# Tokens and weights of a matmul: their distance modulo 256 bytes, and the order of the chunks, made to change from block to block

## The chip, the cores and the metric

The kernel runs on one core of one Trainium2 chip. The metric is device time in microseconds (us) of one execution; lower is better. A core has a matrix engine (TensorE, PE in the profile; its weight loads are listed apart as PEld), a vector engine (VectorE, DVE), an activation engine (ScalarE, ACT), a general engine (GpSimd, POOL) and a queue engine (SyncE, SP), which issues most of the transfers from the chip's memory (HBM) into the on-chip memory SBUF. SBUF has 128 partitions; all addresses below are byte addresses within a partition.

## The reference

One inference step of a decoder layer over 256 prompt tokens and 8 sample tokens, 264 columns in all, with a model width of 2048:

```python
xn = rmsnorm(x, g_mix);  z = xn @ w_in                      # 2048 -> 5128
y_rg = rmsnorm(rglru(conv(z...)) * gelu(z...))               # recurrent group
y_ml = rmsnorm(mlstm(q, k, v, i, f)) * sigmoid(z...)         # matrix-memory group
x = x + concat([y_rg, y_ml]) @ w_out
q = rmsnorm(x) @ w_xa_q;  k, v = mn @ w_xa_k, mn @ w_xa_v    # mn = rmsnorm(mem_prompt), prompt alone
x = x + attention(q, k, v) @ w_xa_o                          # samples use a cache of keys and values
x = x + (silu(xf @ w_ffn_gate) * (xf @ w_ffn_up)) @ w_ffn_down   # xf = rmsnorm(x), width 5632
y = rmsnorm(x)
```

Inputs and outputs are float32. Nearly all the arithmetic is in the products with the weight matrices.

## The kernel before

Activations lie transposed: features on the partitions, 264 tokens along the free dimension. A product with 2048 inputs and 128 outputs is a **block** or step: 16 chunks of 128 inputs, summed in one PSUM bank. To keep float32 precision from the matrix engine's faster float32r format, both operands are split into a high and a low part, and `mm3` (lines 179 to 184) issues three matmuls for each chunk: high weights by high tokens, high weights by low tokens, low weights by high tokens. The weights are the stationary operand (128 columns, loaded anew for each matmul) and the tokens the moving one (264 columns). A block is therefore 48 matmuls.

The list `steps` (line 137) holds all the blocks in order: `w_in`, `w_out`, `w_q`, then for each of 4 heads four blocks of `w_k` and four of `w_v`, then `w_o`, and the feed-forward, which comes in three parts (gate and up blocks in turn, `w_gu`, then 16 down blocks, `w_d`; the last part's down blocks have 12 chunks). `load_piece` (142) loads a block's weights, 1 MB as one transfer, into one of three `raw` buffers of 2048 elements. `split_half` (150) makes the high and low parts of one half, 8 chunks: ScalarE copies `raw` to `wh` with rounding to float32r, VectorE subtracts it from `raw` into `wl`. Both `wh` and `wl` have four buffers of 1024 elements, so two blocks' worth. The buffer of a half is free for a later half when the matrix engine has read all of its chunks.

Token arrays are made by `Arr` (110): four chunks to a tile `[128, 4, 264]` of the shared pool `B`, high and low parts in arrays of their own (`HL`). One chunk is 1056 bytes, which is 4 x 256 + 32, and a tile 4224 bytes, which is 16 x 256 + 128. A chunk of weights in `wh` or `wl` is 512 bytes, two times 256.

Around the blocks, other work (gates, recurrences, the samples' attention over the cache, `dec_k` and `dec_v`) is issued by generators that `pump` runs after each block, on VectorE, ScalarE and GpSimd; results of a block are taken from PSUM in the next step (`pend` in the main loop, 1233 to 1268). A scheduler orders the instructions of each engine; the transfers of SP stay in the order in which they are written.

Of the kernel before, what the change touches and what calls it, by code (L numbers as in the profile page):

```python
# [10 lines left out]
F32 = mybir.dt.float32  # L11
F32R = mybir.dt.float32r
# [5 lines left out]
P = 128  # L18
# [62 lines left out]
def layer_kernel(ctx: ExitStack, tc, xT, memT, vec, wrg, w_in, w_out, w_q, w_k, w_v, w_o,  # L81
# [10 lines left out]
    ctx.enter_context(tc.manual_schedule(engines={mybir.EngineType.SP}))  # L92

    uid = [0]

    def nm(s):
# [10 lines left out]
    def ltmp(w=N):  # L107
        return tmp(w, "lt")

    class Arr:  # L110


# [24 lines left out]
    steps = []  # L137
    LD, LS = 3, 1

    raws, splits = {}, {}  # L140

    def load_piece(i):
        if i >= len(steps) or i in raws:
            return
        src, cols = steps[i][0], steps[i][1]
        r = sb.tile([P, 2048], F32, tag="raw", bufs=3, name=nm("raw"))
        sp.dma_start(r[:, :cols], src)
        raws[i] = r

    def split_half(i, h, parts=1):  # L150
        if i >= len(steps):
            return
        if steps[i][2] is pe_if:
            if h == 0:
                split_gates(i)
            return
        cols = steps[i][1]
        lo, hi = h * 1024, min(cols, (h + 1) * 1024)
        wh = sb.tile([P, 1024], F32R, tag="wh", bufs=4, name=nm("wh"))
        wl = sb.tile([P, 1024], F32R, tag="wl", bufs=4, name=nm("wl"))  # L160
        r = raws[i]
        n = (hi - lo) // parts
        with tc.high_priority():
            for o in range(0, hi - lo, n):
                st["split"] = act.activation(wh[:, o: o + n], r[:, lo + o: lo + o + n], AF.Copy)
                dve.tensor_sub(wl[:, o: o + n], r[:, lo + o: lo + o + n], wh[:, o: o + n])
        splits[i, h] = (wh, wl)

    class W:
        def __init__(self, i):  # L170
            self.i = i

        def __call__(self, c, w=P):
            per = 1024 // w
# [60 lines left out]
    def bank(tag="mm"):  # L235
        return psm.tile([P, 512], F32, tag=tag, bufs=4, name=nm(tag))

    warm_act = const.tile([P, 1], F32, name="warm_act")
    act.activation(warm_act, ones[:, 0:1], AF.Square)

    def warm(n, w=None):
# [263 lines left out]

    def split_gates(i):

        r = raws[i]
        for h in range(2):
            w = sb.tile([P, 8, P], F32R, tag="wh", bufs=4, name=nm("wh"))  # L510
            x = r[:, h * 1024: h * 1024 + 1024].rearrange("p (c m) -> p c m", m=P)
# [610 lines left out]
    for h in range(H):  # L1122
        for j in range(4):
            proj(w_k[4 * h + j], rm, evac_k(h, j), n=T, need=("memg",))
        for k4 in range(4):
            steps.append((w_v[h, k4], 2048, pe_v(h, k4), evac_vm(h) if k4 == 3 else None, ()))

    def ro(c):
        return st["o"](c)
# [6 lines left out]
    def pe_o(m):  # L1136
        def f(i):
            ps = bank()
            w = W(i)
            if m >= 2:  # L1140
                for c in range(KC):
                    mm3(ps[:, :N], w(c), ro(c), c == 0, c == KC - 1)
                return ps
            held[m] = (ps, w)
            for c in range(12):
                mm3(ps[:, :N], w(c), ro(c), c == 0, False)
            if m == 0:
# [17 lines left out]
        return g  # L1165

    for m in range(KC):
        steps.append((w_o[m], 2048, pe_o(m), evac_xo(m), (("att", 2), "dk", "dv") if m == 0 else ()))


# [40 lines left out]
    def load_x(lo, hi):  # L1211
        sp.dma_start(xres[:, lo:hi, :], xT[:, lo:hi, :])

    r = sb.tile([P, 2048], F32, tag="raw", bufs=3, name=nm("raw"))
    raws[0] = r
    for h in range(4):
        if h < 2:
            load_x(2 * h, 2 * h + 2)
        sp.dma_start(r[:, h * 512: h * 512 + 512], w_in[0][:, h * 512: h * 512 + 512])
    for q in range(1, 4):  # L1220
        load_x(4 * q, 4 * q + 4)
        if q < 3:
# [157 lines left out]
```

## Time and profile before

| | before |
|---|---|
| median of 3 runs | 1575.6 us (1570.88 to 1576.71) |
| profiled execution: time | 1576.51 us |
| its span | 1574.8 us |
| granted clock of the matrix engine, mean | 0.991 |
| PE busy, instructions | 1556.5 us, 12340 |
| DVE busy | 1051.4 us |
| ACT busy | 789.7 us |
| read from HBM | 312.78 MB |

The profile's page lists, for one execution, the busy time of each engine, the time line in 40 slices, the transfer queues, the chain of work that ended last (followed back from the last instruction), and the costliest groups of instructions. Matmuls are pipelined: a matmul of 264 columns is listed with a duration of 285 ns, though the next begins some 121 ns after it. What counts for the matrix engine is therefore the time from start to start, which is read from a stretch and the number of matmuls in it.

### The profile page before, as it was taken

Reading aid. Unit: us, or ns where it says so; the run is one execution under the profiler, and the core shown is the slowest. Engines: PE = TensorE matmul, PEld = TensorE weight load, DVE = VectorE, ACT = ScalarE, POOL = GpSimd, SP = SyncE. Lnnn points to the kernel's source line nnn. Section 1 sums busy time; section 2 is a strip of 40 time slices with the busy share of each in tenths; the row PEclk is TensorE's granted clock in tenths of the full one; section 3 lists DMA queues with packets and bytes.
Section 4 is the critical chain, followed back from the end, with each engine's and each line's share of the span. In section 5 each row is a group of like instructions: output and inputs, shape, how many; then the busy total and the mean of one; then the engine's idle time right before and its main releaser. Section 6 shows DMA issues by size and latency. Waiting matters only on the chain.

```text
span 1574.8 us, 29829 instructions
## 1 busy us (share of the span) xinstructions
PE 1556.5 (99%) x12340; PEld 1532.6 (97%) x12340; DVE 1051.4 (67%) x2021; ACT 789.7 (50%) x1252; POOL 109.6 (7%) x174
## 2 busy tenths in 40 slices
PE   9999999999999999999999999999999999999997
PEld 8999999999999889999999999999999999999997
DVE  7876877787699899956655555455555554555554
ACT  7465675565455656645444444333444433344463
POOL 0001210000124333200000000000000000000000
PEclk9999999999999999999999999999999999999998
DMA  8455875546689788745545555555455554555452
GB/s 304 161 174 172 294 269 205 178 145 245 248 321 346 302 305 319 251 161 178 187 164 185 188 180 175 181 188 186 174 179 186 187 181 172 184 188 184 156 179 99
DMA packets 55303, 325.97 MB, mean 207 GB/s; under 512 B 6688, under 2 KB 7120, under 8 KB 24448
## 3 DMA queue, kind: packets, MB, share of 16 engines
q1 hardware_dynamic: 39744, 270.68, 48.4%
q0 software_dynamic: 15136, 53.16, 9.4%
q8 instruction: 96, 1.57, 0.4%
q14 instruction: 39, 0.32, 0.1%
q10 hardware_dynamic: 288, 0.23, 0.1%
HBM read 312.78 MB, written 11.28 MB: 206 GB/s over the span
## 4 chain that ended last, share of the span: by engine, by line
PE 94%; DMA 2%; DVE 2%; ACT 1%; issue 1%; DVEq 0%; POOL 0%; SPq 0%; ACTq 0%
PE mm L60 89%; PE ax L60 4%; DVE B L60 1%; DMA o_sc<-B 1%; ACT B L60 1%; DMA raw<-w_in 1%; ACT wh L60 0%; DMA B<-scr 0%; DVE wl L60 0%; ACT L60 0%; DMA vecs<-vec 0%; DMA scr<-lt 0%; DVE t L60 0%; DVE dw L60 0%; ACT t L60 0%
## 5 line engine op out<-in xcount | busy, mean ns | idle before, releaser
L60 PE MATMUL mm<-B,wh 128*128 128x264 f32 (+1 forms) x7520 | 1379.0, 285 | 4.8 <-DVE B L60 3.0
L60 PEld LDWEIGHTS mm<-B,wh 128*128 128x128 f32 x7520 | 1168.4, 189 | 6.4 <-ACT cso L60 3.1
L60 PE MATMUL mm<-B,wl 128*128 128x264 f32 (+1 forms) x3744 | 1062.8, 284 | 0.6 <-DVE wl L60 0.6
L60 ACT ACTIVATE wh<-raw 128x1024 fp32r<-128x1024 f32 (+2 forms) x518 | 536.9, 1038 | 692.0 <-PE mm L60 574.6
L60 DVE TENSOR_TENSOR wl<-raw,wh 128x1024 fp32r<-128x1024 f32 (+2 forms) x516 | 619.0, 1201 | 356.7 <-ACT wh L60 350.0
L60 PEld LDWEIGHTS mm<-B,wl 128*128 128x128 f32 x3744 | 706.7, 189 | 1.1 <-DVE wl L60 1.0
L60 DVE TENSOR_TENSOR t<-mm,rstd 128x264 f32<-128x264 f32 x104 | 44.9, 432 | 60.2 <-PE mm L60 60.2
L60 PE MATMUL mm<-wh,B 128*128 128x512 f32 x256 | 82.3, 395 | 0.0
L60 DVE TENSOR_TENSOR xres<-xres,mm 128x264 f32<-128x264 f32 x80 | 34.2, 428 | 47.1 <-PE mm L60 47.1
L1272 POOL TENSOR_TENSOR B<-B,rstd 128x264 f32<-128x264 f32 x4 | 2.8, 743 | 864.9 <-ACT rstd L60 864.9
L60 PEld LDWEIGHTS mm<-wh,B 128*128 128x128 f32 x256 | 47.8, 189 | 9.8
L60 DVE SCALAR_TENSOR_TENSOR B<-B,dw 128x256 f32<-128x256 f32 x128 | 52.6, 465 | 2.3 <-ACT dw L60 2.3
L60 PE MATMUL mm<-wl,B 128*128 128x512 f32 x128 | 50.6, 395 | 0.0
L60 DVE SCALAR_TENSOR_TENSOR dw<-B,qsm,dw 128x256 f32<-128x256 f32 x96 | 47.9, 500 | 1.4 <-ACT dw L60 0.7
L60 PE MATMUL ax<-B,B 128*128 128x256 f32 (+3 forms) x288 | 48.2, 308 | 0.3 <-DVE B L60 0.3
L60 PEld LDWEIGHTS ax<-B,B 128*128 128x128 f32 x288 | 40.8, 189 | 4.0 <-issue 1.2
L977 POOL TENSOR_TENSOR ds<-dw,ds 128x256 fp32r<-128x256 f32 x32 | 35.4, 1107 | 115.3 <-ACT ds L60 115.2
L60 ACT ACTIVATE B<-xres,vecs 128x264 fp32r<-128x264 f32 (+1 forms) x64 | 31.1, 503 | 2.5 <-DMA xres<-xT 1.4
L60 ACT ACTIVATE t<-xres 128x264 f32<-128x264 f32 x60 | 23.9, 413 | 15.4 <-DVE xres L60 15.4
L60 PEld LDWEIGHTS mm<-wl,B 128*128 128x128 f32 x128 | 24.1, 188 | 5.0
L966 POOL DMA_DIRECT2D B<-kcT x32 | 17.5, 546 | 147.4 <-DVE B L60 127.0
L60 DVE TENSOR_TENSOR acc_x<-acc_x,t 128x264 f32<-128x264 f32 x59 | 25.2, 428 | 0.9 <-ACT t L60 0.5
(157 smaller groups left out, 740.0 us busy)
## 6 DMA issues: line engine op xcount, KB each, us to landing
raw<-w_gu SPq DMA_DIRECT2D x88, 1024.0 KB, 4.8
raw<-w_in SPq DMA_DIRECT2D x40, 1024.0 KB, 4.9
raw<-w_d SPq DMA_DIRECT2D x32, 1024.0 KB, 4.8
raw<-w_out SPq DMA_DIRECT2D x16, 1024.0 KB, 4.8
B<-kcT POOLq DMA_DIRECT2D x32, 512.0 KB, 6.1
raw<-w_q SPq DMA_DIRECT2D x16, 1024.0 KB, 5.0
B<-vcT POOLq DMA_DIRECT2D x32, 512.0 KB, 7.2
raw<-w_k SPq DMA_DIRECT2D x16, 1024.0 KB, 6.4
```

Source lines behind the costliest of these rows:

```text
L60: return f(*a, **k)
L966: pool_e.dma_start(kc, kcT[h, b])
L977: pool_e.tensor_sub(ws[:, 1], acc, ws[:, 0].bitcast(F32))
L1272: e.tensor_mul(st["y"](c), st["y"](c), r)
```

## The change

In words:

- A half of a block now has one tile `w` of 2176 elements (four buffers) in place of `wh` and `wl`. It is used with a row of 264 elements for each chunk, 1056 bytes as for the tokens: elements 0 to 127 of a row are the high part, 128 to 255 the low part, which is 512 bytes on. The tokens' tiles are 1088 elements (4352 bytes, 17 x 256), and every second tile of an array begins 32 elements later, so that chunk after chunk goes on at 1056 bytes modulo 256. So the distance of a token chunk to its weights modulo 256 bytes is one number for a whole block.
- `scanned` lists the blocks of 16 chunks by 264 columns that wait for nothing of their own: 191 of them, counted in order from 0 (4, 8, 8 and 8 of `w_in`, 15 of `w_out`, 15 of `w_q`, 14 of `w_o`, 31, 32 and 24 of `w_gu`, 16 and 16 of `w_d`). For number k, `place` gives three values: a stride of the chunks (1 for k below 64, 7 below 128, then 3), an offset `a = k // 8 % 8` in units of 32 bytes for the weights, and a rotation `j = k % 8`: the low part of chunk c lies in row (c + j) modulo 8. `order` gives the chunks as stride x k modulo 16.
- Because of the rotation the subtraction of a half is cut in two where j is not 0.
- `w_k` and `w_v` blocks (`wide`) keep 1024 high elements in a row, with the low ones 1056 elements after the start. Blocks that are not scanned use a = 0, j = 0 and the plain order.
- Weights are loaded in halves of 512 KB, into five `raw` buffers of 1024 elements (before: three of 2048).

```diff
+    BW = 4 * N + 32
+    WO, WW = 48, 8 * N + 64
...
         def tile(self, q):
             if q not in self.t:
-                self.t[q] = B([P, min(4, self.nb), self.w], self.dt)
+                t, o = B([P, BW], self.dt), 32 * (q % 2) if self.w == N else 0
+                self.t[q] = t[:, o: o + 4 * self.w].rearrange("p (c n) -> p c n", n=self.w)
...
-        r = sb.tile([P, 2048], F32, tag="raw", bufs=3, name=nm("raw"))
-        sp.dma_start(r[:, :cols], src)
-        raws[i] = r
+        raws[i] = []
+        for o in range(0, cols, 1024):
+            r = raw_half()
+            w = min(1024, cols - o)
+            sp.dma_start(r[:, :w], src[:, o: o + w])
+            raws[i].append(r)
+
+    def raw_half():
+        return sb.tile([P, 1024], F32, tag="raw", bufs=5, name=nm("raw"))
...
-        wh = sb.tile([P, 1024], F32R, tag="wh", bufs=4, name=nm("wh"))
-        wl = sb.tile([P, 1024], F32R, tag="wl", bufs=4, name=nm("wl"))
+        nch = min(8, steps[i][1] // P - 8 * h)
+        w = sb.tile([P, WW], F32R, tag="w", bufs=4, name=nm("w"))
+        if i in wide:
+            wh, wl = w[:, 0: 1024], w[:, 1056: 2080]
...
+        wh, wl = wrows(w, i)
+        r = raws[i][h].rearrange("p (c m) -> p c m", m=P)
+        n = nch // parts
         with tc.high_priority():
-            for o in range(0, hi - lo, n):
-                st["split"] = act.activation(wh[:, o: o + n], r[:, lo + o: lo + o + n], AF.Copy)
-                dve.tensor_sub(wl[:, o: o + n], r[:, lo + o: lo + o + n], wh[:, o: o + n])
+            for o in range(0, nch, n):
+                k = slice(o, o + n)
+                st["split"] = act.activation(wh[:, k], r[:, k], AF.Copy)
+                j = place(i)[2]
+                for u, v in ((o, min(o + n, 8 - j)), (max(o, 8 - j), o + n)):
+                    if u < v:
+                        q = (u + j) % 8
+                        lo = w[:, 8 * place(i)[1]: 8 * place(i)[1] + 8 * N]
+                        lo = lo.rearrange("p (c n) -> p c n", n=N)[:, q: q + v - u, P: 2 * P]
+                        dve.tensor_sub(lo, r[:, u: v], wh[:, u: v].bitcast(F32))
+
+    def wrows(w, i):
+        a, j = place(i)[1:]
+        w = w[:, 8 * a: 8 * a + 8 * N].rearrange("p (c n) -> p c n", n=N)
+        lo = w[:, :, P: 2 * P]
+        return w[:, :, 0: P], [lo[:, (c + j) % 8] for c in range(8)]
+
+    def place(i):
+        k = scanned.index(i) if i in scanned else 0
+        return (1, 7, 3, 5)[k // 64], k // 8 % 8, k % 8
+
+    def order(i):
+        return [place(i)[0] * k % KC for k in range(KC)]
...
-            for c in range(nch):
-                mm3(ps[:, :n], w(c), rhs(c), c == 0, c == nch - 1)
+            for k, c in enumerate(order(i) if nch == KC and i not in wide else range(nch)):
+                mm3(ps[:, :n], w(c), rhs(c), k == 0, k == nch - 1)
             return ps
+        if cols == 2048 and n == N and not need:
+            scanned.append(len(steps))
...
             if m >= 2:
-                for c in range(KC):
-                    mm3(ps[:, :N], w(c), ro(c), c == 0, c == KC - 1)
+                for k, c in enumerate(order(i)):
+                    mm3(ps[:, :N], w(c), ro(c), k == 0, k == KC - 1)
```

More of the change, by code (lines that the diff above doesn't have):

```diff
@@ L94, in layer_kernel @@
     uid = [0]
+    pad = sb.tile([P, 16], F32, tag="pad", bufs=1, name="pad")
     def nm(s):
@@ L138, in layer_kernel @@
     LD, LS = 3, 1
-    raws, splits = {}, {}
+    raws, splits, wide, scanned = {}, {}, set(), []
     def load_piece(i):
@@ L173, in __call__ @@
         def __call__(self, c, w=P):
+            if w == P and self.i not in wide:
+                wh, wl = splits[self.i, c // 8]
+                return wh[:, c % 8], wl[c % 8]
             per = 1024 // w
@@ L236, in bank @@
         return psm.tile([P, 512], F32, tag=tag, bufs=4, name=nm(tag))
-    warm_act = const.tile([P, 1], F32, name="warm_act")
+    warm_act = pad[:, 0:1]
     act.activation(warm_act, ones[:, 0:1], AF.Square)
@@ L506, in split_gates @@
     def split_gates(i):
-        r = raws[i]
         for h in range(2):
-            w = sb.tile([P, 8, P], F32R, tag="wh", bufs=4, name=nm("wh"))
-            x = r[:, h * 1024: h * 1024 + 1024].rearrange("p (c m) -> p c m", m=P)
+            w = wrows(sb.tile([P, WW], F32R, tag="w", bufs=4, name=nm("w")), i)[0]
+            x = raws[i][h].rearrange("p (c m) -> p c m", m=P)
             with tc.high_priority():
@@ L1124, in layer_kernel @@
             proj(w_k[4 * h + j], rm, evac_k(h, j), n=T, need=("memg",))
+            wide.add(len(steps) - 1)
         for k4 in range(4):
             steps.append((w_v[h, k4], 2048, pe_v(h, k4), evac_vm(h) if k4 == 3 else None, ()))
+            wide.add(len(steps) - 1)
     def ro(c):
@@ L1167, in layer_kernel @@
     for m in range(KC):
+        if m >= 2:
+            scanned.append(len(steps))
         steps.append((w_o[m], 2048, pe_o(m), evac_xo(m), (("att", 2), "dk", "dv") if m == 0 else ()))
@@ L1212, in load_x @@
         sp.dma_start(xres[:, lo:hi, :], xT[:, lo:hi, :])
-    r = sb.tile([P, 2048], F32, tag="raw", bufs=3, name=nm("raw"))
-    raws[0] = r
+    raws[0] = [raw_half(), raw_half()]
     for h in range(4):
@@ L1218, in layer_kernel @@
             load_x(2 * h, 2 * h + 2)
-        sp.dma_start(r[:, h * 512: h * 512 + 512], w_in[0][:, h * 512: h * 512 + 512])
+        sp.dma_start(raws[0][h // 2][:, h % 2 * 512: h % 2 * 512 + 512], w_in[0][:, h * 512: h * 512 + 512])
     for q in range(1, 4):
```

9 lines of the change are left out of this document (5 added, 4 removed).

## The prediction

> **What bounds the kernel now.** I read the page first, then the chain of waits in order of time, then stages and single instructions. The page:
>
> ```profile
> span 1574.8 us, 29829 instructions
> PE 1556.5 (99%) x12340; PEld 1532.6 (97%) x12340; DVE 1051.4 (67%) x2021; ACT 789.7 (50%) x1252; POOL 109.6 (7%) x174
> ...
> PE 94%; DMA 2%; DVE 2%; ACT 1%; issue 1%; DVEq 0%; POOL 0%; SPq 0%; ACTq 0%
> ```
>
> The matrix engine is 94% of the chain that ended last; VectorE is 2% of it though it works 67% of the span, so nearly all of its work is covered. The next view is that chain in order of time (start, length, what, how many):
>
> ```profile
> 95.31 5.85 PE mm L60 x48
> ...
> 434.49 5.81 PE mm L60 x48
> ...
> 707.09 91.15 PE mm L60 x750
> ...
> 805.90 754.69 PE mm L60 x6233
> ```
>
> From 805.90 us to the end of the blocks the engine waits for nothing: 754.69 us / 6233 = 121.1 ns for a matmul. The other pieces give 121.9 (5.85 / 48), 121.0 (5.81 / 48) and 121.5 ns (91.15 / 750). So the kernel's time is a count of matmuls times a pace, and what the change can move is the pace. Is it even? One stretch of matmuls in a feed-forward block (start, duration, line, operands, count; starts matter here):
>
> ```profile
> 902.12 0.28 PE L60 MATMUL mm<-B,wl 128*128 128x264 f32 x1
> 902.24 0.41 PE L60 MATMUL mm<-B,wh 128*128 128x264 f32 x2
> 902.48 0.28 PE L60 MATMUL mm<-B,wl 128*128 128x264 f32 x1
> 902.61 0.41 PE L60 MATMUL mm<-B,wh 128*128 128x264 f32 x2
> 902.85 0.29 PE L60 MATMUL mm<-B,wl 128*128 128x264 f32 x1
> 902.98 0.41 PE L60 MATMUL mm<-B,wh 128*128 128x264 f32 x2
> 903.23 0.28 PE L60 MATMUL mm<-B,wl 128*128 128x264 f32 x1
> 903.35 0.40 PE L60 MATMUL mm<-B,wh 128*128 128x264 f32 x2
> 903.59 0.28 PE L60 MATMUL mm<-B,wl 128*128 128x264 f32 x1
> ```
>
> Each low-weight matmul (wl) closes a chunk of three. From one to the next pass 0.36, 0.37, 0.38 and 0.36 us, with no wait between. A chunk of tokens is 1056 bytes and a chunk of weights 512, so here the distance modulo 256 moves on by 32 bytes from chunk to chunk, and eight chunks have seen all eight distances. Placement may therefore matter, by hundredths of a microsecond in a chunk, and the kernel before already takes the mean over all distances in every block (0.363 us, three times 121.1 ns).
>
> **The change part by part.**
>
> *The distance.* 191 blocks of 48 are scanned: 9168 matmuls, 3056 chunks. Each block now holds one distance, but over 64 blocks the offset a takes its eight values eight times each and the rotation j as well; 191 is two such rounds and all but one block of a third. So the first of each chunk's three pairings (high tokens streaming while high weights load) again meets every distance equally often, and the second (low tokens, low weights) does so through j. The kernel before had these two either equal or 128 bytes apart for most arrays; now they stand in any relation, and the third pairing, over to the next chunk, is one of three steps away. No row shows those relations by themselves, so the price has bounds. Near ones: the pieces above, which have different arrays of tokens and so different relations, run from 121.0 to 121.9 ns; against 121.1 that is -0.1 to +0.8 ns, times 9168 = -1 to +7 us. Far ones: all chunks like the shortest shown, (0.36 - 0.363) x 3056 = -9 us, or like the longest, (0.38 - 0.363) x 3056 = +52 us. I take 0: 119 of the 191 blocks lie in the feed-forward, where the 121.1 was read, and an average over eight distances replaces an average over the same eight. One row speaks directly on distances that stay fixed. In a block of `w_k` the tokens' chunks are 1024 bytes and the weights' 512, so it already has one distance throughout:
>
> ```profile
> 559.89 0.28 PE L60 MATMUL mm<-B,wl 128*128 128x256 f32 x1
> 560.00 0.40 PE L60 MATMUL mm<-B,wh 128*128 128x256 f32 x2
> 560.24 0.28 PE L60 MATMUL mm<-B,wl 128*128 128x256 f32 x1
> 560.36 0.40 PE L60 MATMUL mm<-B,wh 128*128 128x256 f32 x2
> 560.59 0.28 PE L60 MATMUL mm<-B,wl 128*128 128x256 f32 x1
> ```
>
> There a chunk takes 0.35 us twice, for 256 columns. Scaled by 264 / 256 that is 0.361 us, the pace of the mixed blocks: holding a distance fixed gains nothing by itself. The blocks that are not scanned (some 30, at a = 0) get one distance too; 1,300 matmuls by the near bounds are under 1 us. `w_k` and `w_v` change their one distance: 1,150 matmuls, likewise.
>
> The Trainium skill says (TensorE: Matmul & The Clock Gate, "Wait — 56ns, not 53.3ns?") that warm matmuls start one after the other at N / 2.4 GHz plus about 2.5 ns; for 264 columns this is 112.5 ns, an estimate from that page, 8.6 ns under the 121.1 that the trace shows, so the trace is not at that pace. Were it reached in all scanned blocks, the sum would be 79 us lower, near 1499; by the row it stays at 121.1.
>
> *The cut subtractions.* 167 of the 191 blocks have j above 0, and each of their two halves is subtracted in two pieces: 334 more VectorE instructions. These rows are of one feed-forward step (VectorE, then ScalarE):
>
> ```profile
> 901.29 1.06 ACT L60 ACTIVATE wh<-raw 128x1024 fp32r<-128x1024 f32 x1 [1.46 <-PE mm L60]
> 904.21 1.06 ACT L60 ACTIVATE wh<-raw 128x1024 fp32r<-128x1024 f32 x1 [1.86 <-PE mm L60]
> ...
> 902.38 1.23 DVE L60 TENSOR_TENSOR wl<-raw,wh 128x1024 fp32r<-128x1024 f32 x1 [1.31 <-ACT wh L60]
> 904.27 0.43 DVE L60 TENSOR_TENSOR t<-mm,rstd 128x264 f32<-128x264 f32 x1 [0.67 <-PE mm L60]
> ```
>
> 1.23 us for 1024 elements and 0.43 for 264 give 1.05 ns an element and 0.15 us for an instruction. 334 x 0.15 = 50 us of VectorE work. VectorE is on the chain for 2% of the span, 31 us of its 1051 (3%), hardly any of it in the feed-forward; 3% of 50 is 1.5 us. Bounds: 0, if all is covered, and 8 us if the 28 scanned blocks of `w_in` (24 with a cut, 2 cuts each, 0.15 us = 7 us), where VectorE is on the chain, all show. I take 1.5. The cover elsewhere is VectorE's idle time, which is least here:
>
> ```profile
> 450.00:500.00 50.00, 50.00 (x418) 50.00 (x417) 46.70 (x127) 27.91 (x48) 17.27 (x26) 1.00 0.90 337
> 500.00:550.00 50.00, 49.87 (x330) 45.52 (x330) 44.19 (x110) 30.15 (x56) 14.48 (x21) 1.00 0.84 333
> 1000.00:1200.00 200.00, 200.00 (x1654) 200.00 (x1653) 107.03 (x123) 80.30 (x90) 0.00 (x0) 1.00 0.52 182
> ```
>
> (Columns: stretch, length, busy of PE, PEld, DVE, ACT, POOL with counts, clock, transfer share, GB/s.) In the `w_q` blocks VectorE has 46.70 of 50 us; 8 blocks there add some 2 us, which still fits. If it did not, the samples' attention would end later, by those microseconds; nothing waits for it before `w_o`.
>
> *The order of the chunks.* Strides 7 and 3 begin with block 64, the seventh of the 14 in `w_o`; then both halves of a block stay in use to its end. Before, the first half's buffer came free in mid-block: the two ScalarE rows above, 2.9 us apart, are the releases at the middle and at the end. Now both come at the end, and what is queued is: two copies (1.06 each), two subtractions (1.23 + 0.15 each) behind the first copy, and ahead of these up to three products of 0.43 on VectorE. 1.06 + 2 x 1.38 = 3.8 us, or 5.1 with all three products in the way, while the block takes 5.81. So the next halves are ready 0.7 to 2 us early: cost 0. If that cover went, the matrix engine would wait at the first chunks of each of 127 blocks.
>
> *The halved loads.* 256 more issues on SP, and five half buffers for six. From the waits of SP's queue (us in total, times, longest), its time line and the table of transfers (KB each, us to landing):
>
> ```profile
> SPq L147 <- DVE wl L60: 872.5, 154, 18.2
> ...
> 2.19 1.38 SPq L1219 DMA_DIRECT2D raw<-w_in  x3
> ...
> raw<-w_gu SPq DMA_DIRECT2D x88, 1024.0 KB, 4.8
> raw<-w_k SPq DMA_DIRECT2D x16, 1024.0 KB, 6.4
> ```
>
> An issue takes 1.38 / 3 = 0.46 us, so 256 of them 118 us of a queue that waits 872 us for a buffer alone. With one half buffer less, the second half of a load starts half a block (2.9 us) later. A load lands in 4.8 us, 6.4 where `w_k` competes with the cache, and is asked for up to two blocks ahead (11.6 us): 11.6 - 2.9 - 6.4 = 2.3 us in hand. Cost 0; if that went, the late subtractions below are what would follow.
>
> **The sum**, against the profiled execution's own 1576.5 us (0.9 above the median of 1575.6): 0 + 1.5 + 0 + 0 gives 1578.
>
> **The rivals.**
>
> *Slower: the relations that were not there before are slow ones.* The pace would rise in the scanned blocks from the first `w_in` block on. If their mean chunk took 0.37 us, as one of the four shown, that is 0.007 x 3056 = +21 us, 1599; it decides once the mean is 0.003 us above 0.363 (8 us). For it: chunks of 0.37 and 0.38 exist, and a block that holds a slow distance repeats it 16 times. Against it: every distance comes equally often, and the four pieces, with different relations, stay within 0.9 ns.
>
> *Faster: a distance that holds lets the streams settle.* At 0.36 us a chunk the scanned blocks save 9 us, 1569 with the cut subtractions. For it: two of the four chunks shown take 0.36. Against it: the fixed distance of `w_k` shows 0.361 after scaling, and the slow half of the distances is in the scan too.
>
> *Slower: halves ready too late under strides 7 and 3.* It decides when VectorE has over 5.81 - 3.8 = 2.0 us of other work ahead of the subtractions in a block; 1.3 is what I count. At 0.3 us late in 127 blocks it gives +38 us, 1616.
>
> *Slower: the loads*, in the stretch from 450 to 550 us, where transfers run at 337 and 333 GB/s: 0.5 us in each of its 17 blocks (100 / 5.8) would be +9 us, 1587.
>
> *The change does nothing to the pace.* Then the sum is the same 1578 and the unevenness shown has another cause, such as the tokens' own addresses. The Trainium skill has such a rule (TensorE: Matmul & The Clock Gate, "Step-by-step: what each phase is for"): moving operand and weights come through two independent read ports, and loading the next weights takes nothing from the running matmul. By it no distance could matter; the trace's 0.36 to 0.38 us without a wait between does not agree fully, though it does not show that the weights are the cause.
>
> **How the numbers follow.** 0.5% (8 us) is about what a measurement of this kernel can tell from no change. The pace unchanged, by averaging or because the distance does not matter: 0.56, with a time of 1570 to 1584. Faster: 0.16. Slower pace 0.18, late halves 0.06, loads 0.04, together 0.28. The predicted time is that of the first case, 1578. The range from 1566 to 1592 holds that case, nearly all of the faster one and the lower half of the slower pace (to 0.368 us a chunk, +14 us); outside stay the late halves and the slow end, and a pace below any shown.
>
> **What would show it.** Right: in the chain of waits, long pieces of PE in the feed-forward with 121.1 ns as their mean, but uneven from block to block: stretches of 46.5 us (eight blocks) would hold now more, now fewer than 384 matmuls. VectorE busy 1051 + 50 = about 1100 us. No idle time of PE put down to `w` after 300 us. Wrong: a mean pace of 122 ns or more, or 120 or less, in that stretch; or waits of PE for VectorE's or ScalarE's `w` at each block from the ninth of `w_o` on; or a start that is later than the 805.90 of the last long piece by much more than 1.5 us.

## The result, and the profile after

| | before | after |
|---|---|---|
| median of 18 runs each | 1573.24 us (1570.88 to 1576.98) | 1578.61 us (1577.40 to 1582.79) |
| ratio to before | 1 | 1.0034, interval 1.0026 to 1.0041 |
| profiled execution: time | 1576.51 us | 1577.61 us |

The changed kernel is 5.4 us slower, 0.34%: a difference that its interval tells from zero, though it is under the 0.5% that the prediction took for about the least that a measurement of this kernel can tell. The predicted time of 1578 was reached. The two profiled executions differ by only 1.1 us, because the one of before lay 3.3 us above the median of its runs and the one of after 1.0 us below. The sizes below therefore come from the ratios of the runs, and the traces are used for where the time goes.

The page of the kernel after: span, busy engines, shares of the chain of waits, the group of the subtractions (with the busy time and the mean in ns after the bar), and two rows of the table of transfers.

```profile
span 1575.9 us, 31045 instructions
PE 1556.6 (99%) x12340; PEld 1532.3 (97%) x12340; DVE 1056.5 (67%) x2355; ACT 775.2 (49%) x1252; POOL 109.2 (7%) x174
...
PE 94%; DVE 2%; DMA 1%; ACT 1%; issue 1%; SPq 0%; POOL 0%; DVEq 0%; ACTq 0%
...
L60 DVE TENSOR_TENSOR w<-raw,w 128x1024 fp32r<-128x1024 f32 (+7 forms) x852 | 634.4, 787 | 126.5 <-ACT w L60 125.4
...
raw<-w_gu SPq DMA_DIRECT2D x176, 512.0 KB, 4.1
...
raw<-w_k SPq DMA_DIRECT2D x32, 512.0 KB, 4.9
```

The picture is that of before: the matrix engine is 94% of the chain. VectorE has 334 more instructions (2355 for 2021) and only 5.1 us more busy time. Half a load lands in 4.1 us where a whole one took 4.8.

The chain of waits of the kernel after, in order of time (start, length, what, how many):

```profile
100.88 5.86 PE mm L60 x48
...
429.67 5.91 PE mm L60 x48
...
703.81 92.57 PE mm L60 x759
...
802.59 759.13 PE mm L60 x6236
```

This is where the time is. In the last piece a matmul takes 759.13 / 6236 = 121.73 ns, 0.65 ns more than the 121.08 ns of before (754.69 / 6233); in the piece ahead of it 92.57 / 759 = 121.96 for 121.53. The last piece begins 3.3 us *earlier* than before. So there is a loss in the pace, and something else that may gain; how much is left to the runs, since the profiled execution of before was itself 3.3 us slower than the median.

Is the pace uneven from block to block, as forecast? A down block's result is added to `xres` by VectorE as soon as the matrix engine releases it, so the starts of these additions are a clock of the blocks (VectorE's time line of after; start, duration, operation, then the idle time before it and what ended it; only the additions are shown):

```profile
1024.98 0.43 DVE L60 TENSOR_TENSOR xres<-xres,mm 128x264 f32<-128x264 f32 x1 [2.64 <-PE mm L60]
...
1030.84 0.43 DVE L60 TENSOR_TENSOR xres<-xres,mm 128x264 f32<-128x264 f32 x1 [2.73 <-PE mm L60]
...
1036.73 0.43 DVE L60 TENSOR_TENSOR xres<-xres,mm 128x264 f32<-128x264 f32 x1 [2.61 <-PE mm L60]
...
1042.53 0.43 DVE L60 TENSOR_TENSOR xres<-xres,mm 128x264 f32<-128x264 f32 x1 [2.58 <-PE mm L60]
...
1048.39 0.43 DVE L60 TENSOR_TENSOR xres<-xres,mm 128x264 f32<-128x264 f32 x1 [2.58 <-PE mm L60]
...
1054.13 0.43 DVE L60 TENSOR_TENSOR xres<-xres,mm 128x264 f32<-128x264 f32 x1 [2.48 <-PE mm L60]
...
1059.88 0.43 DVE L60 TENSOR_TENSOR xres<-xres,mm 128x264 f32<-128x264 f32 x1 [2.47 <-PE mm L60]
```

From one to the next pass 5.86, 5.89, 5.80, 5.86, 5.74 and 5.75 us. In the same stage of before the step is even:

```profile
1026.31 0.43 DVE L60 TENSOR_TENSOR xres<-xres,mm 128x264 f32<-128x264 f32 x1 [0.71 <-PE mm L60]
...
1032.13 0.43 DVE L60 TENSOR_TENSOR xres<-xres,mm 128x264 f32<-128x264 f32 x1 [0.71 <-PE mm L60]
...
1037.95 0.43 DVE L60 TENSOR_TENSOR xres<-xres,mm 128x264 f32<-128x264 f32 x1 [0.71 <-PE mm L60]
```

Twice 5.82 us. Read from the start times of the matmuls block by block, 168 blocks of the kernel after have a mean pace of 121.7 ns, and single blocks lie between 119.7 and 125.9. By the stride of the chunks the means are 121.7 (1), 121.8 (7) and 121.7 (3). So the blocks differ now, and their mean is above the pace of before. The experiments ask three things: whether it is really the place of the weights; what the halved loads and the cuts gave; and why the mean is not the pace of before.

### The profile page after: what moved, and what is told of

The parts are those of the page before. It is cut to its first block, busy times and chain, and to the rows that moved or that the text cites. A ratio compares the mean times of both kernels' runs of the same rounds, so it can differ in the third digit from the quotient of the medians.

```text
span 1575.9 us, 31045 instructions
## 1 busy us (share of the span) xinstructions
PE 1556.6 (99%) x12340; PEld 1532.3 (97%) x12340; DVE 1056.5 (67%) x2355; ACT 775.2 (49%) x1252; POOL 109.2 (7%) x174
## 4 chain that ended last, share of the span: by engine, by line
PE 94%; DVE 2%; DMA 1%; ACT 1%; issue 1%; SPq 0%; POOL 0%; DVEq 0%; ACTq 0%
PE mm L60 89%; PE ax L60 5%; DVE B L60 1%; DVE w L60 1%; ACT B L60 1%; DMA B<-scr 0%; ACT w L60 0%; DMA o_sc<-B 0%; DMA xres<-xT 0%; DMA scr<-lt 0%; DVE t L60 0%; ACT L60 0%; ACT t L60 0%; DVE c L60 0%; DVE dw L60 0%
## 5 line engine op out<-in xcount | busy, mean ns | idle before, releaser
L60 PE MATMUL mm<-B,w 128*128 128x264 f32 (+1 forms) x11264 | 1388.2, 285 | 5.2 <-DVE B L60 2.2
L60 PEld LDWEIGHTS mm<-B,w 128*128 128x128 f32 x11264 | 1377.0, 189 | 7.3 <-ACT cso L60 2.3
L60 ACT ACTIVATE w<-raw 128x1024 fp32r<-128x1024 f32 (+2 forms) x518 | 522.9, 1034 | 682.8 <-issue 409.1
L60 DVE TENSOR_TENSOR w<-raw,w 128x1024 fp32r<-128x1024 f32 (+7 forms) x852 | 634.4, 787 | 126.5 <-ACT w L60 125.4
L60 DVE TENSOR_TENSOR xres<-xres,mm 128x264 f32<-128x264 f32 x80 | 34.2, 427 | 121.7 <-PE mm L60 121.6
L60 PE MATMUL mm<-w,B 128*128 128x512 f32 x384 | 93.3, 395 | 0.0
L60 PEld LDWEIGHTS mm<-w,B 128*128 128x128 f32 x384 | 70.4, 188 | 15.2
L1013 POOL DMA_DIRECT2D B<-kcT x32 | 17.5, 548 | 143.4 <-DVE B L60 122.4
L60 ACT ACTIVATE B<-t 128x264 fp32r<-128x264 f32 x44 | 18.4, 417 | 18.1 <-DVE t L60 18.1
L60 DVE SCALAR_TENSOR_TENSOR B<-xres,vecs,B 128x264 fp32r<-128x264 f32 x48 | 22.6, 487 | 4.7 <-ACT B L60 4.7
L60 ACT ACTIVATE t<-B,B 128x128 f32<-128x128 f32 x64 | 21.5, 390 | 6.7 <-DMA B<-scr 6.7
L60 ACT ACTIVATE t<-t 128x264 f32<-128x264 f32 (+1 forms) x61 | 24.7, 405 | 0.1
```

The lines of the kernel that those rows point to most:

```text
L60: return f(*a, **k)
L1013: pool_e.dma_start(kc, kcT[h, b])
```

## The experiments

The ratios are to the kernel before, run on the same chip beside each. A kernel's pace is given from the last long piece of its chain of waits unless the text says otherwise.

### Does the distance matter?

The theory: a block's pace is set by where its weights lie against its tokens, modulo 256 bytes, and by the order of the chunks. The rival: the pace belongs to the tokens' own addresses or to the stage, and a distance does nothing. Three kernels hold one place for all scanned blocks. The first two differ from each other in nothing but the weights' addresses (192 bytes); the tokens lie where they lay. The third changes only the order of the chunks; some token tiles get other buffers by it, at the same distances modulo 256.

**One place, 192 bytes** (against the kernel after):

```diff
-        return (1, 7, 3, 5)[k // 64], k // 8 % 8, k % 8
+        return (1, 6, 0) if i in scanned else (1, 0, 0)
```

> The kernel after with one place for all 191 scanned blocks: stride 1, a = 6 (weights 192 bytes on), j = 0. In the trace of after the one block with these three values ran at 119.8 ns a matmul, against 121.7 as the mean of all blocks. Theory A (the distance of tokens and weights modulo 256 sets the pace): 9168 x (119.8 - 121.7) = -17 us against after, so about 1561 us, and under the kernel before (1573) by about 12. Theory B (the pace hangs on the tokens' own addresses or on which array is read; weights and tokens do not disturb each other): the tokens lie as in after, so 1576 to 1580 us.

**One place, 0 bytes, plain order:**

```diff
-        return (1, 7, 3, 5)[k // 64], k // 8 % 8, k % 8
+        return 1, 0, 0
```

> One place for all blocks: stride 1, a = 0, j = 0. It differs from the stride 7 run in the order of the chunks alone, and from the run with a = 6 in the weights' place alone (192 bytes). Blocks of the trace of after with these values ran at 121.4 to 122.5 ns. Theory A: 1576 to 1586 us. Theory B: the same as the run with a = 6, within 3 us.

**The same place, stride 7:**

```diff
-        return (1, 7, 3, 5)[k // 64], k // 8 % 8, k % 8
+        return (7, 0, 0) if i in scanned else (1, 0, 0)
```

> One place for all scanned blocks: stride 7, a = 0, j = 0. Its one block in the trace of after was the slowest of all, 125.9 ns a matmul. Theory A: 9168 x (125.9 - 121.7) = +39 us against after, about 1617 us. Theory B: 1576 to 1580 us. If halves that become free late under stride 7 cost anything, waits of PE for w at each block's beginning show it, over and above the pace.

Measured: 192 bytes 1560.01 us, ratio 0.9909 (0.9895 to 0.9923); 0 bytes 1574.34 us, 1.0002 (0.9993 to 1.0011); 0 bytes with stride 7 1622.90 us, 1.0313 (1.0298 to 1.0328). The last pieces of their chains, and two of the additions to `xres` in each, first at 192 bytes:

```profile
797.77 747.28 PE mm L60 x6232
```

```profile
1010.03 0.43 DVE L60 TENSOR_TENSOR xres<-xres,mm 128x264 f32<-128x264 f32 x1 [0.56 <-PE mm L60]
...
1015.78 0.43 DVE L60 TENSOR_TENSOR xres<-xres,mm 128x264 f32<-128x264 f32 x1 [0.55 <-PE mm L60]
```

at 0 bytes in plain order:

```profile
802.62 756.66 PE mm L60 x6232
```

```profile
1006.10 0.43 DVE L60 TENSOR_TENSOR xres<-xres,mm 128x264 f32<-128x264 f32 x1 [0.59 <-PE mm L60]
...
1011.92 0.43 DVE L60 TENSOR_TENSOR xres<-xres,mm 128x264 f32<-128x264 f32 x1 [0.59 <-PE mm L60]
```

and at 0 bytes with stride 7:

```profile
825.13 784.96 PE mm L60 x6236
```

```profile
1024.98 0.43 DVE L60 TENSOR_TENSOR xres<-xres,mm 128x264 f32<-128x264 f32 x1 [2.99 <-PE mm L60]
...
1031.04 0.43 DVE L60 TENSOR_TENSOR xres<-xres,mm 128x264 f32<-128x264 f32 x1 [2.99 <-PE mm L60]
```

The pace is 119.9, 121.4 and 125.9 ns, a block 5.75, 5.82 and 6.06 us. Moving the weights by 192 bytes is worth 14.3 us of the kernel, and the order of the chunks alone 48.6 us. The rival falls. What these runs move is the weights; no run moves the tokens alone by a chosen amount, so whether the distance counts or the weights' own addresses do is not shown. Of the 48.6 us not quite all is pace: the scanned blocks by themselves have 126.25 and 121.40 ns, (126.25 - 121.40) x 9168 = 44.5 us. The other 4 us are waits: with stride 7 from the first `w_in` block on, the matrix engine waits 3.5 us in all for VectorE's `w`, four times, where the plain order has 1.3 us, once, and 4.0 for 2.2 us for VectorE's `B`.

### The halved loads and the cut subtractions

The prediction had 0 and 1.5 us for these. **The halved loads alone, in the kernel before:**

```diff
-        r = sb.tile([P, 2048], F32, tag="raw", bufs=3, name=nm("raw"))
-        sp.dma_start(r[:, :cols], src)
-        raws[i] = r
+        raws[i] = []
+        for o in range(0, cols, 1024):
+            r = raw_half()
+            w = min(1024, cols - o)
+            sp.dma_start(r[:, :w], src[:, o: o + w])
+            raws[i].append(r)
+
+    def raw_half():
+        return sb.tile([P, 1024], F32, tag="raw", bufs=5, name=nm("raw"))
...
```

> The kernel before with the halved loads alone (512 KB into five half buffers). In after, the last long piece of the chain begins 3.3 us earlier than in before (802.6 for 805.9), where 1.5 us later was forecast. If the halved loads are what shortens the first 800 us: 3 to 4 us under the kernel before, about 1570, with the last long piece beginning near 802.5. If they are neutral and the gain comes from the tiles or from the order that the scheduler makes of them: 1573, within 1.5 us, and the piece at 805 to 806.

Measured: 1570.79 us, ratio 0.9980 (0.9971 to 0.9989), a gain of 0.2%. Its chain:

```profile
800.29 754.59 PE mm L60 x6233
```

The pace is that of before (121.06 ns); the gain is in the start of the piece. Compared by ratios it is 0.0020 x 1573 = 3.1 us, by its median and that of the kernel before beside it (1573.23) 2.4.

**The cuts alone, in the kernel before** (every half of a 2048-column block is subtracted in two pieces, 256 and 768 columns, 478 more instructions):

```diff
-                dve.tensor_sub(wl[:, o: o + n], r[:, lo + o: lo + o + n], wh[:, o: o + n])
+                cut = 256 if parts == 1 and cols == 2048 else n
+                for u, v in ((o, o + cut), (o + cut, o + n)):
+                    if u < v:
+                        dve.tensor_sub(wl[:, u: v], r[:, lo + u: lo + v], wh[:, u: v])
```

> The kernel before with the subtractions of all blocks of 2048 columns cut in two (256 and 768 of 1024 elements): 478 more VectorE instructions, all else as it was. The prediction gave 3% of 0.15 us an instruction to the path: 478 x 0.15 x 0.03 = 2 us, so 1575. If VectorE's work is covered throughout: 1573, within 1 us. If all cuts in the w_in blocks show: 36 blocks x 2 x 0.15 = 11 us, 1584. VectorE's busy time tells what a cut costs it.

Measured: 1582.75 us, 1.0045 (1.0028 to 1.0062), from six runs of which two lie near 1578 us and four between 1582 and 1584. But this does not price the cuts, because the edit did more than one thing: the pace changed with it.

```profile
809.50 756.53 PE mm L60 x6233
```

It is 121.37 ns against 121.08, though the matmuls are untouched. The edit gave buffers other addresses: in the program as built, 7904 of the 10592 matmuls of weights by 264 columns stream their tokens from another place. That this set the pace is likely, but it was not tried by itself. So the cuts were tried again where the place is held, **in the kernel with one place at 0 bytes** (each scanned half cut 2 chunks to 6, 382 more instructions):

```diff
-                for u, v in ((o, min(o + n, 8 - j)), (max(o, 8 - j), o + n)):
+                t = o + 2 if i in scanned else o + n
+                for u, v in ((o, t), (t, o + n)):
```

> The run with one place at a = 0 (1574.3 us) with each subtraction of the 191 scanned blocks cut in two (2 and 6 chunks): 382 more VectorE instructions, the same places, so the same pace of 121.4. This is the cost of the cuts without the change of pace that the cut kernel before had from its buffers' new places (121.35 for 121.03). If all that kernel's 9 us beyond 3 us of pace are the cuts: 6 x 382 / 478 = 5 us, 1579. If 3% of 0.15 us a cut reach the path, as predicted: 1576. VectorE's busy time should rise by 0.07 x 382 = 27 us.

Measured: 1576.15 us, 1.0010 (1.0001 to 1.0018), against 1.0002 (0.9993 to 1.0011) without the cuts. That is 0.0008 x 1573 = 1.3 us, with intervals that overlap: between nothing and some 3 us. Its pace is unchanged, 756.66 / 6232. The pages of both, with the cuts:

```profile
PE 1554.2 (99%) x12340; PEld 1529.7 (97%) x12340; DVE 1076.6 (68%) x2403; ACT 787.5 (50%) x1252; POOL 107.8 (7%) x174
```

and without them:

```profile
PE 1556.7 (99%) x12340; PEld 1533.5 (97%) x12340; DVE 1050.7 (67%) x2021; ACT 787.7 (50%) x1252; POOL 108.2 (7%) x174
```

VectorE has 25.9 us more work for 382 instructions: 0.07 us for a cut.

### Why is the mean over the distances not the pace of before?

Before, nearly every block went through all eight distances (159 of 192 in the program as built; a tile of tokens is 128 bytes off a multiple of 256, so its four chunks can repeat the distances of the four ahead of them, and 33 blocks met only four), and its pace was 121.1 ns. After, the blocks have one distance each and the mean over them is 121.7. What is different? The first theory was the rotation: before had the high and the low pairing in fixed relations, after sets them in any. **Without rotation** (offsets of 32 bytes, plain order):

```diff
-        return (1, 7, 3, 5)[k // 64], k // 8 % 8, k % 8
+        return 1, k % 8, 0
```

> The kernel after with stride 1 and j = 0 throughout, a = k modulo 8: all three pairings of a chunk stand in relations that the kernel before had too, but each block holds one distance. No subtraction is cut. If the 0.6 ns that after lost a matmul come from relations that before did not have (low tokens to low weights by j): the mean is back at 121.1, and with the halved loads' gain the time is 1571 to 1573 us. If they come from holding one distance, or from rows of 1056 bytes for the weights: the mean stays at 121.7, and the time is 1576 to 1578. Block by block: 119.7 at a = 6, 121.4 at a = 0, as in the runs with one place.

Measured: 1579.16 us, 1.0034 (1.0021 to 1.0047). The theory falls: the kernel stays as slow as the one after. Its chain:

```profile
802.56 761.03 PE mm L60 x6232
```

122.1 ns. From the start times in its blocks, the paces at the eight offsets are:

| offset, bytes | 0 | 32 | 64 | 96 | 128 | 160 | 192 | 224 |
|---|---|---|---|---|---|---|---|---|
| ns a matmul | 121.6 | 121.1 | 124.1 | 123.0 | 124.6 | 120.7 | 119.8 | 121.8 |

Next theory: holding a distance is itself what costs. **Rows of 1088 bytes for the weights** put 32 bytes back between one chunk and the next (downwards, 1056 - 1088, where before it was upwards, 1056 - 2 x 512), with one place for all blocks (`split_half` places the low weights by the same rows):

```diff
-        w = w[:, 8 * a: 8 * a + 8 * N].rearrange("p (c n) -> p c n", n=N)
+        w = w.rearrange("p (c n) -> p c n", n=N + 8)
...
-        return (1, 7, 3, 5)[k // 64], k // 8 % 8, k % 8
+        return 1, 0, 0
```

> Rows of 272 elements (1088 bytes) for the weights instead of 264, one place, stride 1, j = 0: the distance again moves on by 32 bytes from chunk to chunk, through all eight in each block, with the tiles, loads and splits of after. If holding one distance is what makes the mean over places 121.7 to 122 (runs with a scan) and not 121.1 (before): pace near 121.1, time 1571 to 1573 us. If the weights' interleaved rows cost the 0.6 to 0.9 ns whatever the distance does: 121.7 to 122, 1576 to 1580 us.

Measured: 1583.41 us, 1.0062 (1.0044 to 1.0080), the slowest of these apart from the fixed place with stride 7. Its chain:

```profile
802.52 762.68 PE mm L60 x6232
```

122.4 ns. A distance that moves through all eight values is no guarantee of 121.1, so this theory falls too, at least as the whole answer. Is 32 bytes the grain at all? **Offsets in steps of 4 bytes**, 64 places (in `split_half` likewise):

```diff
-        w = w[:, 8 * a: 8 * a + 8 * N].rearrange("p (c n) -> p c n", n=N)
+        w = w[:, a: a + 8 * N].rearrange("p (c n) -> p c n", n=N)
...
-        return (1, 7, 3, 5)[k // 64], k // 8 % 8, k % 8
+        return 1, k % 64, 0
```

> As the run without rotation, but the weights move by 4 bytes from block to block (k modulo 64 elements): all 64 places in 256 bytes, three blocks for each. If the pace hangs on the distance in steps of 32 bytes or coarser, places between two multiples of 32 run at the pace of one of them, and the fastest of all is 119.7 ns as at 192 bytes. If finer steps matter, paces differ within 32 bytes, perhaps below 119.7. Mean 121 to 122 ns, time 1572 to 1580 us. Were it the alignment of the weights to 16, 32 or 64 bytes and not the distance, places off the alignment would all be slower by the same.

Measured: 1578.01 us, 1.0025 (1.0016 to 1.0035). The blocks' clock in its down blocks:

```profile
1001.28 0.43 DVE L60 TENSOR_TENSOR xres<-xres,mm 128x264 f32<-128x264 f32 x1 [0.60 <-PE mm L60]
...
1007.26 0.43 DVE L60 TENSOR_TENSOR xres<-xres,mm 128x264 f32<-128x264 f32 x1 [0.67 <-PE mm L60]
1013.14 0.43 DVE L60 TENSOR_TENSOR xres<-xres,mm 128x264 f32<-128x264 f32 x1 [0.61 <-PE mm L60]
1018.97 0.43 DVE L60 TENSOR_TENSOR xres<-xres,mm 128x264 f32<-128x264 f32 x1 [0.59 <-PE mm L60]
...
1024.74 0.43 DVE L60 TENSOR_TENSOR xres<-xres,mm 128x264 f32<-128x264 f32 x1 [0.57 <-PE mm L60]
```

Neighbouring blocks, whose weights lie 4 bytes apart, take 5.98, 5.88, 5.83 and 5.77 us. Over the 64 places the pace goes from 119.2 ns (124 bytes) to 124.7 (172 bytes), with a mean of 121.8. The three blocks at 124 bytes agree to 0.02 ns. 24 bytes gives 120.3 and 28 bytes 122.8; 128 bytes, next to the 119.2 of 124, gives 124.1 here and 124.6 in the scan before. So the grain is 4 bytes or finer, and no simple rule (32-byte steps, alignment) orders the values.

But the place is not all. Here are 47 matmuls of three blocks whose weights lie at 64 bytes, from the matrix engine's time line (start, time from the first one's start to the last one's end, count), two of the run without rotation:

```profile
807.60 5.82 PE L60 MATMUL mm<-B,w 128*128 128x264 f32 x47
...
854.32 6.02 PE L60 MATMUL mm<-B,w 128*128 128x264 f32 x47
```

and one of the run in 4-byte steps:

```profile
842.72 5.87 PE L60 MATMUL mm<-B,w 128*128 128x264 f32 x47
```

In the programs as built, the three blocks have the same addresses, of weights and of tokens alike, and the granted clock is 1.00 in all three. Without the 0.285 us of the last matmul, 46 steps take 120.3, 124.7 and 121.4 ns each. What differs is what ran ahead: a block that six small matmuls with the identity had interrupted, a block at 32 bytes, and a block at 60 bytes. (The 124.1 of the table is a mean over such blocks.) Nor is this the only such case. In the feed-forward, blocks at 160 bytes take 120.7 ns in the one scan and 122.6 in the other. So a block's pace depends on its place and, at least at some places, on what the engine did just before; how that is carried over was not tried. Within one scan each place has the same place ahead of it in nearly every round, and so its values repeat.

Does the low pairing count as much as the high one? **High weights held at 124 bytes, low weights in 64 places** (`r` is the fourth value of `place`; in `split_half` likewise):

```diff
-        a, j = place(i)[1:]
-        w = w[:, 8 * a: 8 * a + 8 * N].rearrange("p (c n) -> p c n", n=N)
-        lo = w[:, :, P: 2 * P]
+        a, j, r = place(i)[1:]
+        w = w[:, a: a + 8 * N].rearrange("p (c n) -> p c n", n=N)
+        lo = w[:, :, P + r: 2 * P + r]
...
-        return (1, 7, 3, 5)[k // 64], k // 8 % 8, k % 8
+        return 1, 31, k % 64 // 8, k % 8
```

> High weights at 124 bytes throughout, low weights at 64 places in steps of 4 bytes (row by j, column by 0 to 7), three blocks for each. If the pairing of low tokens and low weights matters as much as that of the high ones, paces spread from about 118.5 to 124 ns round a mean near 121; the place with no shift is 119.2 again. If the high pairing alone decides, all stay near 119.2.

Measured, in a single run: 1578.01 us. In its blocks, with the place of the low weights alone moving from block to block, the pace goes from 119.2 to 123.7 ns, with a mean of 121.8. So it does.

Last theory: the layout has nothing to do with the 0.6 ns; the place that before happened to have was a good one, and a scan over places has a mean of 121.7 to 122 in any layout. **The kernel before with halved loads, and its high and low weights moved 4 bytes from block to block** (rows of 512 bytes and the order of before):

```diff
-        wh = sb.tile([P, 1024], F32R, tag="wh", bufs=4, name=nm("wh"))
-        wl = sb.tile([P, 1024], F32R, tag="wl", bufs=4, name=nm("wl"))
...
+        s = scanned.index(i) % 64 if i in scanned else 0
+        wh = sb.tile([P, 1088], F32R, tag="wh", bufs=4, name=nm("wh"))[:, s: s + 1024]
+        wl = sb.tile([P, 1088], F32R, tag="wl", bufs=4, name=nm("wl"))[:, s: s + 1024]
```

> The kernel before with the halved loads, and with high and low weights of a scanned block moved by 4 bytes from block to block (64 places, three blocks each). Chunks of weights stay 512 bytes apart, so the distance moves on by 32 bytes from chunk to chunk, as in before. If chunks 512 bytes apart are what holds before at 121.0 ns (an average over eight distances in a block, whatever the place): all 64 places lie within some 0.5 ns of 121.0, time 1570 to 1573 us. If before's place is only a better one among many, as 0 bytes was among those of the runs with a scan: places spread from about 120 to 123 round a mean of 121.8, time 1577 to 1580 us.

Measured: 1577.40 us, 1.0018 (1.0009 to 1.0028), against 0.9980 for the same kernel with its weights in one place: 0.0038 x 1573 = 6.0 us, by nothing but the place (the tiles of the weights are 256 bytes longer, which leaves their starts modulo 256 as they were). Its chain:

```profile
800.78 758.31 PE mm L60 x6233
```

121.66 ns. The 64 places spread less here (about 121.0 to 122.5), since each block goes through eight distances, and the place of before, offset 0, is at 121.04 among the lowest. That is the answer as far as the runs go: moving the weights from block to block costs the layout of before its advantage, the mean of the even scan is that of the other scans, and it was before that lay under it. What stays open is how much of the 0.6 ns the other places cost and how much the moving itself, since what ran ahead counts too. In the feed-forward, 0 bytes takes 121.4 ns where it is held, 121.5 in the 32-byte scan and 122.5 in the 4-byte scan; 192 bytes takes 119.7, 119.8 and 120.2; 124 bytes 119.2, held and scanned.

### One chosen place for all blocks

The 64 places give a candidate that beats both kernels: **every block that isn't `w_k` or `w_v` at 124 bytes** (offsets in elements as above):

```diff
-        k = scanned.index(i) if i in scanned else 0
-        return (1, 7, 3, 5)[k // 64], k // 8 % 8, k % 8
+        return 1, 31, 0
```

> One place for every block but those of w_k and w_v: stride 1, weights 124 bytes on, j = 0. Its three blocks among the 64 places of four-byte steps were the fastest, 119.2 ns each within 0.01. If a block's pace is a fixed property of its place: 9168 x (119.2 - 121.7) = -23 us against after, and some 2 us more from the blocks that were not scanned: 1552 to 1556 us, 4 to 8 under the run at 192 bytes. If the pace of single blocks in a scan owes something to the blocks around it: no better than 1560.

Measured: 1551.21 us (1550.85 to 1553.37), ratio 0.9857 (0.9842 to 0.9872): 22.5 us under the kernel before, some 27 under the one after. Its chain and its windows (stretch, length, then busy time and count of PE, PEld, DVE, ACT and POOL, the granted clock, the transfers' share, GB/s):

```profile
697.13 89.61 PE mm L60 x751
...
794.33 743.15 PE mm L60 x6232
```

```profile
1000.00:1200.00 200.00, 200.00 (x1681) 200.00 (x1680) 110.04 (x129) 82.01 (x94) 0.00 (x0) 1.00 0.55 185
```

119.25 ns, at a granted clock of 1.00, and 1681 matmuls in the 200 us that held 1654 before. The gain of the one place that was found in 4-byte steps carries over to the whole kernel. This was worth a run: at 160 bytes, say, the two scans would have promised different things.

## Why the prediction was right, and where it was not

The total was right, 1578 forecast and 1578.6 measured. Part of that is the base: the sum started from the profiled execution, 3.3 us above the later median, and forecast a change of +1.5 where +5.4 was measured. That the two totals lie 0.6 us apart is luck: a base 3.3 us too high and a gain of 2.4 us from the loads that was left out stand against a pace that was put 5.7 us too low. The terms:

- **The distance, "I take 0".** Wrong: this term was mis-sized. The runs show +0.6 ns on 9168 matmuls, 5.5 to 6 us, near the upper end of the near bounds (+7). The step that failed is "an average over eight distances replaces an average over the same eight". Two averages over the same distances needn't agree: the eight-offset scan without rotation gave 122.1, the one with 1088-byte rows 122.4, before 121.1. The pace depends on the place to 4 bytes, on both pairings, on the order of the chunks and on what ran before, and the place of before was a good one among its neighbours. The near bounds (pieces of the chain, 121.0 to 121.9 ns) held for the mean. Of the far bounds, made from single chunks of 0.36 and 0.38 us, the upper one held for the places that were tried alone: the slowest takes 3 x 126.25 = 0.379 us a chunk. The lower one did not: the best takes 3 x 119.25 = 0.358, and its kernel gains 22.5 us where that bound allowed 9.
- **"Holding a distance fixed gains nothing by itself".** Right, and by no means the whole matter: held places reach from 119.2 to 126.3 ns. The row of `w_k` on which it stood was one place among them (0.361 us a chunk, read to two places, is 120.3 ns a matmul).
- **The cut subtractions, 1.5 us.** Right in size (1.3, from nothing to some 3, for 382 of them; 334 were in the change), by two errors that cancel. The records of the single subtractions bear out the 0.15 us of the sum (0.952 and 0.425 us for two pieces, 1.226 for a whole half), but subtractions that follow one another overlap, so a cut adds 0.07 us of busy time. The same overlap saves some where the two halves of a block are subtracted one straight after the other, as with strides 7 and 3; so busy time is 1056.5 and not "about 1100". Meanwhile the share of the cuts on the path was some 5% (1.3 of 25.9) and not 3%, as far as the intervals allow. Where it lies is not settled, since the trace with the cuts has its last piece no later than the one without.
- **The order of the chunks, 0.** Right from `w_o` on. Strides 1, 7 and 3 have means of 121.7, 121.8 and 121.7 ns. Both halves are copied together after the end of a block, ScalarE and VectorE of after:

```profile
1059.57 2.02 ACT L60 ACTIVATE w<-raw 128x1024 fp32r<-128x1024 f32 x2 [3.74 <-issue]
...
1060.67 2.50 DVE L60 TENSOR_TENSOR w<-raw,w 128x256 fp32r<-128x256 f32 x4 [0.35 <-ACT w L60]
```

  The subtractions end 3.6 us after the copies begin (1060.67 + 2.50 - 1059.57), as worked out, and the blocks' waits for VectorE's `w` come to one, of 0.8 us, in the whole execution. Where the stride begins in `w_in`, the cover is thinner: that experiment had four such waits, 3.5 us.
- **The halved loads, 0.** Wrong in size. They gain 2.4 to 3 us; the bound was thought out against a loss alone. The gain lies ahead of the last piece; which of the early waits it shortens was not isolated.

Together: +5.7 (pace) - 2.4 (loads) + 1.3 (cuts) = +4.6 of the +5.4 measured; the rest is within the intervals.

The rivals. *Slower relations* named the right mechanism at a size that the mean didn't reach: 0.3652 us a chunk (three times 121.73) is under the point of 0.366 from which it was to decide. A single place reaches it and goes beyond (1622.90). *A distance that holds lets the streams settle* exists for chosen places only; 1560.01 and 1551.21 go beyond the 1569 that it was given. *Late halves* and *the loads* did not come. *The change does nothing to the pace* is refuted, though its time was right: 192 bytes more for the weights were worth 14.3 us. The Trainium skill's rule (TensorE: Matmul & The Clock Gate, "Step-by-step: what each phase is for") has moving operand and weights on two independent read ports; by it a place of the weights could not matter, and the measurement decides against that. The Trainium skill's pace (TensorE: Matmul & The Clock Gate, "Wait — 56ns, not 53.3ns?"), an estimate of 112.5 ns for 264 columns, was not reached either; the lowest of all places tried is 119.2.

Of the signs forecast, the even total and the uneven blocks were right. The stretches of eight blocks were not: both 46.5 us stretches of after hold 384 matmuls.

```profile
900.00:946.50 46.50, 46.50 (x384) 46.50 (x383) 25.96 (x46) 18.57 (x24) 0.00 (x0) 1.00 0.54 180
1060.00:1106.50 46.50, 46.50 (x384) 46.50 (x383) 24.56 (x42) 17.43 (x22) 0.00 (x0) 1.00 0.54 180
```

The rotation changes with each block, so the pace changes with each block, and eight of them are a mean already. The additions to `xres` were the view that shows it.

## What to carry to other kernels

A kernel whose matrix engine never waits still has a pace, and the pace is worth a look: with the same instructions in the same order it went from 119.2 to 124.7 ns from block to block of a scan over the weights' places. An edit that moves buffers, like the cut subtractions here, may come with a change of pace that is larger than what the edit itself costs, so price such an edit with the place held. To use it, let one run scan many places block by block, read each block's time, hold the best one, and run that kernel too, since a block's time in the scan also depends on the block ahead of it. A scan of all places is slower than a layout that happens to be good, and one chosen place was worth 1.4%.

## What the runs showed of the hardware that was not expected

- The time of a float32r matmul of 264 columns with a weight load of its own depends on the place of the weights in SBUF, to 4 bytes or finer (124 bytes 119.2 ns, 128 bytes 124.1). Tried alone, places gave 119.2, 119.7, 121.4 and, with stride 7, 126.3 ns, each at a granted clock of 1.00 in the feed-forward.
- The place does not fix the pace by itself: three blocks with the same addresses took 120.3, 124.7 and 121.4 ns a matmul after different blocks ahead of them. With one place held, at 0 bytes or at 124, the blocks of the feed-forward agree to 0.02 ns.
- High and low pairing count alike: moving the low weights alone covers 119.2 to 123.7 ns.
- The order of the chunks counts at an unchanged place: 121.4 for plain order, 126.3 for stride 7, both at 0 bytes and without rotation. Yet over the places of the kernel after, strides 1, 7 and 3 have the same mean.
- What in the chip makes a place fast or slow stays open. The runs exclude the eight distances of 32 bytes as the whole description, and the holding of a distance as the cause; they don't show whether reads collide, nor which.
